# The sums of w_out made by accumulating DMAs in DRAM in place of VectorE's subtractions through SBUF

## Chip, cores and metric

The kernel runs on one core of one Trainium2 chip. The metric is the device time of one execution in microseconds (us). The kernel before takes 778.07 us (median of three runs, 777.9 to 778.26). A measurement of this kernel can tell a difference of about 0.2% from none.

## What is computed

One layer: a normalisation, a gated short convolution between two matrix products, a second normalisation and the residual. x is 1024 x 1024, w_in 1024 x 8192, w_out 2048 x 1024, all float32.

```python
u = rms_norm(h, pre_norm)
z, bg, cg, v = split(u @ w_in, 4)            # each 1024 x 2048
y = bg * causal_dwconv(cg * v, conv_w) * silu(z)
m = y @ w_out
out = h + rms_norm(m, post_norm)
```

## The kernel before

Both products are made by a scheme of seven products on halves (Strassen's, in Winograd's form): in place of eight half-size products, sums of the quarters of both operands are made, and seven products of those sums are combined. Two of the seven ("b" and "f") are cut once more by the same scheme into seven small ones (a' to g'). The matmuls work on float32 values that are split into a high and a low part: ScalarE writes the high part with a cast, VectorE subtracts it from the value to get the low part, and each product is three matmuls (low by high, high by low, high by high; L226 to L228, L798 to L800, L1138 to L1140, L1234 to L1236).

**First stage.** The 16 blocks c of 128 columns of y are made one after the other. For each there are two weight pairs, p = 2c (cg and v) and p = 2c + 1 (z and bg). The loop over `slots` is the order of the work: slots ("a", p), ("c", p), ("e", p), ("d", p), ("g", p), with the small products of b and f between them. Behind each product, `prepare` splits the weights of the slots to come (7 us ahead by a list of costs), `after` empties the PSUM bank, and further work is hung onto the slot by its name. All of this is written in program order; each engine runs its own instructions in that order (`tc.manual_schedule()`), and waits come from the buffers that instructions read and write.

- SyncE (SP) issues all but one of the DMAs: `fetch` the raw weights (L138), `y_done` the store of y (L291), and loads and stores of sums.
- GpSimd (POOL) makes the sums of the weights, `add_s` (L150 to L158) and `deep_sums` (L752 to L756), and a few multiplications (L260, L827, L1086).
- ACT's `snap` (L234) copies the PSUM bank of product a, c or e to SBUF before the next product is added to the same bank.
- The sums of w_out for the second stage are made on the side, one block j a pair, at p = 8 to 23 (`TODO`). At even p, VectorE makes four sums of the quarters b11, b12, b21, b22 of w_out (`fetch_t`, L330, four loads; `add_t`, L355 and L356, four subtractions and four stores to `t_d`). At odd p, GpSimd makes the sums for the small products of b and f (L326 and L342 to L351).
- SBUF work space is a ring of 36 pages of 128 x 512 float32.

**Second stage** (m = y @ w_out), from about 620 us. `units` of w_out sums (u) and y sums (y) are loaded (`load_unit`, L858), split (`split_pages`, ACT cast and VectorE subtraction at L162 and L163) into a pool of seven buffers "u", and multiplied (`out_mm`). Product "a" comes first (two halves h, four row tiles q), then `product_b` with the small products a', b', c', e', d', f', g' (`small_mm`, L1234 to L1236, and `small_add`, L1241). Around the start of it the program order is this:

1. end of the loop over slots: loads of A2, B3 and X; splits of B2, B1 and **A1**;
2. two more `fetch_unit`, then the loads of `gpost` (L1121), the post-norm weights spread over the partitions, one tile for each half of the columns;
3. products of ("a", 0); y sums on VectorE (L935, L936); `add_y` of the last block (L312 to L314); splits of **A2** and **A3**;
4. products of ("a", 1); split of **B3**; copies of the four banks of "a" to `acc`, that is C11 (L1196, ACT);
5. small products a', b', c', ...; behind each, `small_add` adds its bank to two rows of `acc`. a', c', d' and g' accumulate in one bank, which `small_add` reads after each.

```python
DEEP_C = {"a'": ("x'", 0, 0), "b'": ("y'", 0, 0), "c'": ("x'", 0, 1), ...
OUT_A = {"a'": ("A1", 0), ..., "b'": ("A2", 0), ..., "e'": ("A3", 0), "c'": ("A3", HH)}
OUT_B = {"a'": ("B1", 0), ..., "b'": ("B2", 0), ..., "c'": ("B3", 0), ...}
```

Of the kernel before, what the change touches and what calls it, by code (L numbers as in the profile page):

```python
# [12 lines left out]
ALU = mybir.AluOpType  # L13
# [4 lines left out]
DEEP_F = 3  # L18
# [5 lines left out]
def kernel(  # L24
# [16 lines left out]
    nc = tc.nc  # L41
    P = 128
    _, L, D = x.shape
# [4 lines left out]
    HB = 512  # L48
# [10 lines left out]
    wov = w_out[0].rearrange("(c p) n -> p c n", p=P)  # L59
# [13 lines left out]
    def page(name, dtype=F32, shape=(HB,)):  # L73

        return pages.tile([P, *shape], dtype, tag="pg", name=name, bufs=PAGES)
# [9 lines left out]
    CH = NC // 2  # L85
# [4 lines left out]
    t_d = dram.tile([P, 4, CH, HB], F32, tag="t_d", name="t_d")  # L90

    CQ = CH // 2
    tb_d = dram.tile([P, 2, 2, CQ, HB], F32, tag="tb_d", name="tb_d")
    tx_d = dram.tile([P, 2, CQ, HB // 2], F32, tag="tx_d", name="tx_d")
# [77 lines left out]
    def by_seven(z, c):  # L172

        return c >= DEEP if z == "b" else DEEP_F <= c < NC - 1
# [127 lines left out]
    def add_y(c):  # L302

        if c < CH:
            cv = done.pop(c)
            t = page(f"s3_{c}")
            nc.vector.tensor_sub(t, cv[:, :HB], cv[:, HB:])
            nc.sync.dma_start(s_d[:, SK["d"], c], t)
        else:
            cv, (t0, t1) = done.pop(c), far_y.pop(c)  # L310
            t2 = page(f"s4_{c}")
            nc.vector.tensor_add(t1, t1, cv[:, HB:])  # L312
            nc.vector.tensor_sub(t0, t1, t0)
            nc.vector.tensor_sub(t2, cv[:, :HB], t0)  # L314
            for k, t in zip("cef", (t0, t1, t2)):
                nc.sync.dma_start(s_d[:, SK[k], c - CH], t)

    ts = {}

    def fetch_t(j):  # L320

        if j >= CH:
            z, k = divmod(j - CH, CQ)
            ts[j] = [page(f"tb{n}_{j}") for n in (0, 1)]
            for n in (0, 1):
                nc.sync.dma_start(ts[j][n], wov[:, CH + k + n * CQ, z * HB : (z + 1) * HB])  # L326
            return
        ts[j] = [page(f"t{n}_{j}") for n in range(4)]
        for n, t in enumerate(ts[j]):
            nc.sync.dma_start(t, wov[:, j + n // 2 * CH, n % 2 * HB : (n % 2 + 1) * HB])  # L330

    def add_t(j, steps=range(4)):

        if j >= CH:
            z, k = divmod(j - CH, CQ)
            if 0 in steps:
                ts[j].append(page(f"t23_{j}"))
            b0, b1, t = ts[j]
            l, r = slice(0, HB // 2), slice(HB // 2, HB)
            for n in steps:  # L340
                if n == 0:
                    nc.gpsimd.tensor_sub(b0[:, r], b0[:, r], b0[:, l])  # L342
                    nc.sync.dma_start(tb_d[:, z, 0, k], b0)
                elif n == 1:
                    nc.gpsimd.tensor_sub(t[:, l], b1[:, r], b0[:, r])
                elif n == 2:
                    nc.gpsimd.tensor_sub(t[:, r], t[:, l], b0[:, l])
                    nc.sync.dma_start(tb_d[:, z, 1, k], t)
                else:
                    nc.gpsimd.tensor_sub(b1[:, l], b1[:, l], t[:, l])  # L350
                    nc.sync.dma_start(tx_d[:, z, k], b1[:, l])  # L351
            return
        t = ts[j]
        for n, a, b in [((1, 1, 0), (3, 3, 1), (0, 3, 0), (2, 2, 3))[n] for n in steps]:
            nc.vector.tensor_sub(t[n], t[a], t[b])  # L355
            nc.sync.dma_start(t_d[:, n, j], t[n])  # L356


    idle = small.tile([P, P], F32, tag="idle", name="idle", bufs=1)
# [501 lines left out]
    def fetch_unit():  # L861
        n = len(fetched)
        if n < len(UNITS):
            fetched.append(load_unit(*UNITS[n]))
# [87 lines left out]

    END = len(PAIRS) - 1

    TODO = {2 * DEEP_F + 2 + 2 * j + n: j + n * CH for j in range(CH) for n in (0, 1)}


    slots = [("a", 2), ("b", 2)]
    for p in range(2, len(PAIRS)):
        q = p + 1  # L960
# [35 lines left out]
    at, t = [], 0.0  # L996
# [6 lines left out]
    def prepare(n):  # L1003
        while ready[0] < len(slots) and at[ready[0]] < at[n + 1] + LEAD:
            slot = slots[ready[0]]
            if slot[2:]:
                z, i, c = slot
                deep_prep(z, c, i)
            elif slot[::-1] not in wt:
                split_w(*slot[::-1])  # L1010
            ready[0] += 1

    first_chunk("")
    for n, slot in enumerate(slots):
        if slot[2:]:
            z, i, c = slot
            deep_product(z, c, i)

            early = (z, i) in (("f", "c'"), ("f", "e'"))
            if early:  # L1020
                deep_after_f(c, i)
            if (z, i) != ("f", "c'"):
                prepare(n)
            if z == "f":
                if not early:
                    deep_after_f(c, i)
                continue
            deep_after(c, i)
            if (i, c) == ("f'", NC - 1):
                third_unit(0)  # L1030
            elif i == "g'" and c == NC - 1:
                nc.scalar.activation(sn[2 * c + 1, "a"], sn[2 * c + 1, "a"], AF.Silu)
            continue
        i, p = slot
        f7 = by_seven("f", p // 2)
        product(p, i)

        ahead = DEEP <= (p - (i == "a")) // 2 < DEEP_F and (i, p % 2) in (("d", 1), ("a", 0))
        for step in (after, prepare) if ahead else (prepare, after):
            step(*((n,) if step is prepare else (p, i)))  # L1040
        q, prev = p + 1, p // 2 - 1
        if p == 2:
            first_chunk(i)
        if i == "c":
            if p % 2 and p // 2 < DEEP:
                nc.scalar.activation(sn[p, "a"], sn[p, "a"], AF.Silu)
            if p % 2 == 0 and p in TODO:
                fetch_t(TODO[q])
            if p % 2 == 0 and p > 2:
                fetch_s(prev)  # L1050
            if p % 2 == 0 and p in TODO:
                add_t(TODO[p], [0, 1])
            if p % 2 == 0 and p // 2 >= DEEP:
                deep_sums("b", p // 2, 1)
        elif i == "e":
            add_s(q, "ecdf" if f7 else "ec")
            if f7 and p % 2 == 0:
                for part in (0, 1):
                    deep_sums("f", p // 2, part)
            if p % 2 and q in TODO:  # L1060
                fetch_t(TODO[q])
            if p in TODO and p % 2:
                add_t(TODO[p])
            elif p in TODO:
                add_t(TODO[p], [2, 3])
        elif i == "d":
            if p + 2 <= END:
                fetch(p + 2)
            if not f7:
                add_s(q, "d")  # L1070
            if p % 2 == 0 and p > 2:
                if f7:
                    split_w(q, "c")
                add_y(prev)
        elif i == "f":
            add_s(q, "f")
            if p == 2:
                add_y(0)
        elif i == "g":
            if p % 2 and q <= END and q // 2 >= DEEP:  # L1080
                deep_sums("b", q // 2, 0)
        elif i == "a":
            if p % 2 == 0 and prev >= DEEP:
                for t in (sn[p - 1, "c"], sn[p - 1, "a"]):
                    nc.scalar.activation(t, t, AF.Silu)
                nc.gpsimd.tensor_mul(cvs[prev][:, HB:], sn[p - 1, "c"], sn[p - 1, "e"])  # L1086
        if DEEP < NC and (i, p) in UNDER:
            UNDER[i, p]()
        if p == END - 1 and i in "cd":
            fetch_unit()  # L1090
        if p == END:
            if i in "acg":
                split_unit()
            elif i == "d":
                third_unit(2)
            if i in "ac":
                fetch_unit()
            elif i == "d":
                load_small("b", "B2")
            elif i == "f":  # L1100
                load_small("b", "A1")
                load_small("b", "B1")
                fetch_s(NC - 1)
            elif i == "g":
                for n in ("A2", "B3", "X"):
                    load_small("b", n)
                split_small("b", "B2")
                split_small("b", "B1")
                sums_y("b", "d", nc.vector)
                split_small("b", "A1")  # L1110
# [8 lines left out]
    gpost = [page(f"gpost{e}") for e in range(NE)]  # L1119
    for e in range(NE):  # L1120
        nc.sync.dma_start(gpost[e], post_norm[:, e * HB : (e + 1) * HB].broadcast_to([P, HB]))  # L1121
    acc = p2.tile([P, 2, TH, HB], F32, tag="acc", name="acc")
    jk = p2.tile([P, HB], BF16, tag="jk", name="jk")
    so = small.tile([P, NT, NE], F32, tag="so", name="so", bufs=1)
# [228 lines left out]
```

## Time and profile before

| what | value |
|---|---|
| median of three runs | 778.07 us (777.9 to 778.26) |
| the profiled execution, from its first to its last instruction (span) | 776.2 us; no other time of it is given |
| mean granted clock of TensorE | 0.997 of full speed |
| busy share: TensorE, VectorE, ScalarE, GpSimd | 99%, 80%, 56%, 53% |
| DMA | 127.17 MB, mean 164 GB/s |
| HBM read, written | 91.78 MB, 34.60 MB |

Times in the profile are us from the span's start unless marked ns. PE is TensorE, PEld its weight loads, DVE VectorE, ACT ScalarE, POOL GpSimd, SP SyncE; a q behind a name is that engine's issuing of DMAs and semaphore work, which counts as not busy. A row of a timeline gives start, length (of a run of equal instructions together), engine, line, operation, output and input, shape, the number of instructions and, in brackets, the idle time before and what ended it. A row of waits gives the sum of us, the number of times and the longest. A row of the table of stretches gives, for each engine, its busy time and, in brackets, its instructions, then TensorE's granted clock, the share of the DMA engines' time and GB/s. Matmuls overlap in the records, so the step from one start to the next is the time that each takes, not its recorded length.

### The profile page before, as it was taken

The page shows a single profiled execution, that of the slowest core. Times are in us where ns is not written, and L with a number is a line of the kernel's source. Part 1 is how long each engine was busy: PE and PEld are TensorE (multiplying, and loading weights), DVE is VectorE, ACT ScalarE, POOL GpSimd, SP SyncE. Part 2 cuts the span into 40 slices and gives each one's busy share as a digit, 9 for nine tenths or more (in the row PEclk, how much of TensorE's full clock was granted, in tenths as well). Part 3 has the DMA queues.
Part 4 walks back from the last instruction along what each step waited for, and adds up shares of the span by engine and source line. Part 5 has one row for each costly group of instructions (what it writes and reads, how often), then busy time and mean ns, then how long its engine had stood idle before and what let it go on. Part 6 is the DMA issues. An engine that isn't in the chain of part 4 may idle for free.

```text
span 776.2 us, 12058 instructions
## 1 busy us (share of the span) xinstructions
PE 766.0 (99%) x4086; PEld 661.8 (85%) x4086; DVE 618.4 (80%) x934; ACT 436.3 (56%) x810; POOL 413.2 (53%) x369
## 2 busy tenths in 40 slices
PE   8999999999999999999999999999999999999996
PEld 6888888888888888888888888888888889889985
DVE  5899786778687878788888887676778899966975
ACT  6764354766556565546465556555544576753821
POOL 2506786937575757575767667373737100850041
PEclk9999999999999999999999999999999999999998
DMA  9210531335463637364847456232325989966345
GB/s 310 71 55 1 149 96 55 96 109 181 138 204 117 210 111 230 111 208 131 257 136 250 138 174 178 96 109 96 115 89 166 336 275 378 309 196 210 112 169 184
DMA packets 115965, 127.17 MB, mean 164 GB/s; under 512 B 7432, under 2 KB 74304, under 8 KB 115904
## 3 DMA queue, kind: packets, MB, share of 16 engines
q1 hardware_dynamic: 115888, 126.41, 50.5%
q8 instruction: 32, 0.52, 0.3%
q14 instruction: 29, 0.24, 0.1%
q10 hardware_dynamic: 16, 0.00, 0.0%
HBM read 91.78 MB, written 34.60 MB: 163 GB/s over the span
## 4 chain that ended last, share of the span: by engine, by line
PE 98%; DVE 1%; DMA 1%; ACT 0%; POOL 0%; issue 0%; POOLq 0%; DVEq 0%; ACTq 0%
PE px L226 15%; PE px L227 15%; PE px L228 15%; PE pv L226 4%; PE pv L227 4%; PE pv L228 4%; PE po_x L1139 4%; PE po_x L1140 4%; PE po_x L1138 4%; PE px2b L800 2%; PE px2b L798 2%; PE px2b L799 2%; PE px2f L800 1%; PE px2f L799 1%; PE px2f L798 1%; PE pp L456 1%
## 5 line engine op out<-in xcount | busy, mean ns | idle before, releaser
L260 POOL TENSOR_TENSOR sne<-sne,cv 128x512 f32<-128x512 f32 x15 | 20.5, 1369 | 122.3 <-DVE cv L683 106.4
L187 ACT COPY beside<-raw 128x512 f32<-128x512 f32 x84 | 49.6, 590 | 29.2 <-DVE dwb1l L188 21.7
L154 POOL TENSOR_TENSOR se<-raw,raw 128x512 f32<-128x512 f32 x31 | 46.8, 1510 | 19.2 <-PE px L228 6.8
L234 ACT COPY sna<-px 128x512 f32<-128x512 f32 x30 | 17.6, 588 | 68.8 <-PE px L228 68.1
L226 PE MATMUL px<-u_d,wdl 128*128 128x512 f32 x124 | 48.7, 393 | 0.0
L226 PE MATMUL px<-u_a,wal 128*128 128x512 f32 x124 | 48.6, 392 | 0.0
L227 PE MATMUL px<-u_a,wah 128*128 128x512 f32 x124 | 48.6, 392 | 0.0
L227 PE MATMUL px<-u_d,wdh 128*128 128x512 f32 x124 | 48.5, 391 | 0.0
L226 PE MATMUL px<-u_g,wgl 128*128 128x512 f32 x124 | 48.4, 391 | 0.0
L227 PE MATMUL px<-u_g,wgh 128*128 128x512 f32 x124 | 48.4, 391 | 0.0
L227 PE MATMUL pv<-u_e,weh 128*128 128x512 f32 x124 | 48.4, 390 | 0.0
L228 PE MATMUL px<-u_d,wdh 128*128 128x512 f32 x124 | 48.4, 390 | 0.0
L226 PE MATMUL pv<-u_e,wel 128*128 128x512 f32 x124 | 48.4, 390 | 0.0
L228 PE MATMUL px<-u_a,wah 128*128 128x512 f32 x124 | 48.3, 389 | 0.0
L227 PE MATMUL px<-u_c,wch 128*128 128x512 f32 x124 | 48.2, 389 | 0.0
L228 PE MATMUL px<-u_c,wch 128*128 128x512 f32 x124 | 48.2, 389 | 0.0
L228 PE MATMUL pv<-u_e,weh 128*128 128x512 f32 x124 | 48.2, 389 | 0.0
L226 PE MATMUL px<-u_c,wcl 128*128 128x512 f32 x124 | 48.2, 389 | 0.0
L228 PE MATMUL px<-u_g,wgh 128*128 128x512 f32 x124 | 48.2, 389 | 0.0
L156 POOL TENSOR_TENSOR sc<-se,raw 128x512 f32<-128x512 f32 x31 | 44.9, 1448 | 5.8 <-issue 3.4
L158 POOL TENSOR_TENSOR sf<-raw,sc 128x512 f32<-128x512 f32 x31 | 46.3, 1493 | 0.0
L355 DVE TENSOR_TENSOR t<-t,t 128x512 f32<-128x512 f32 x32 | 45.8, 1450 | 0.3
(539 smaller groups left out, 2743.7 us busy)
## 6 DMA issues: line engine op xcount, KB each, us to landing
raw<-in_sc_w_in SPq DMA_DIRECT2D x128, 256.0 KB, 4.0
y_d<-cv SPq DMA_DIRECT2D x16, 512.0 KB, 3.2
s_d<-s SPq DMA_DIRECT2D x32, 256.0 KB, 2.9
t<-in_sc_w_out SPq DMA_DIRECT2D x32, 256.0 KB, 2.9
t_d<-t SPq DMA_DIRECT2D x32, 256.0 KB, 3.9
tb<-in_sc_w_out SPq DMA_DIRECT2D x16, 256.0 KB, 4.3
s<-y_d SPq DMA_DIRECT2D x16, 256.0 KB, 4.1
xr<-in_x SPq DMA_DIRECT2D x16, 256.0 KB, 3.8
```

The costliest lines, as they stand in the source:

```text
L154: nc.gpsimd.tensor_add(t, block(p, 1, 0), block(p, 1, 1))
L156: nc.gpsimd.tensor_sub(t, sums[p, "e"], block(p, 0, 0))
L158: nc.gpsimd.tensor_sub(t, block(p, 0, 1), sums[p, "c"])
L187: nc.scalar.copy(b, src)
L226: nc.tensor.matmul(ps, lo, UH[i][:, k], start=first and k == 0, stop=False, skip_group_check=True)
L227: nc.tensor.matmul(ps, hi, UL[i][:, k], start=False, stop=False, skip_group_check=True)
L228: nc.tensor.matmul(ps, hi, UH[i][:, k], start=False, stop=last, skip_group_check=True)
L355: nc.vector.tensor_sub(t[n], t[a], t[b])
L798: nc.tensor.matmul(ps, lo, uh, start=first and k == 0, stop=False, skip_group_check=True)
L1138: nc.tensor.matmul(ps, lo, u[:, 0, k], start=first, stop=False, skip_group_check=True)
L1139: nc.tensor.matmul(ps, hi, u[:, 1, k], start=False, stop=False, skip_group_check=True)
L1140: nc.tensor.matmul(ps, hi, u[:, 0, k], start=False, stop=last, skip_group_check=True)
```

## The change

The four sums of w_out for products d, e, g and c are no longer loaded to SBUF and subtracted. Their signs are turned (the second column half of w_out's sums and of the matching y sums change sign), so that e = b11 + b12, d = b12 + b22, c = e + b22 and g = c + b21. For each half h of the blocks there are six steps, one a pair from p = 8 (h = 0) and from p = 14 (h = 1):

- step 0: SP copies b11 to e and b12 to d, inside DRAM (1 MB each); step 2: SP copies e to c; step 4: SP copies c to g;
- step 1: b12 is added to e, and b22 to d, by four accumulating DMAs of 512 KB issued from GpSimd; step 3: b22 to c, two of them; step 5: b21 to g, two of them. They wait in a list `pending`, and `next_sum` issues one behind each slot.

GpSimd's own sums at odd p stay where they were. In `add_y` the three y sums of the far blocks are made with the other sign: a subtraction and two instructions of the form (a * -1) - b. The second half of the output columns comes out with the sign turned; gpost[1] is multiplied by -1 on ScalarE, right behind its load, to turn it back.

```diff
-            nc.vector.tensor_add(t1, t1, cv[:, HB:])
-            nc.vector.tensor_sub(t0, t1, t0)
-            nc.vector.tensor_sub(t2, cv[:, :HB], t0)
+            nc.vector.tensor_sub(t1, cv[:, HB:], t1)
+            nc.vector.scalar_tensor_tensor(t0, t1, -1.0, t0, op0=ALU.mult, op1=ALU.subtract)
+            nc.vector.scalar_tensor_tensor(t2, cv[:, :HB], -1.0, t0, op0=ALU.mult, op1=ALU.subtract)
...
     def fetch_t(j):
...
-        ts[j] = [page(f"t{n}_{j}") for n in range(4)]
-        for n, t in enumerate(ts[j]):
-            nc.sync.dma_start(t, wov[:, j + n // 2 * CH, n % 2 * HB : (n % 2 + 1) * HB])
...
     def add_t(j, steps=range(4)):
...
-        t = ts[j]
-        for n, a, b in [((1, 1, 0), (3, 3, 1), (0, 3, 0), (2, 2, 3))[n] for n in steps]:
-            nc.vector.tensor_sub(t[n], t[a], t[b])
-            nc.sync.dma_start(t_d[:, n, j], t[n])
...
+    pending = []
+
+    def out_sums(step, h):
+
+        js = slice(h * CQ, (h + 1) * CQ)
+        far = slice(CH + h * CQ, CH + (h + 1) * CQ)
+        b11, b12 = (wov[:, js, e * HB : (e + 1) * HB] for e in (0, 1))
+        b21, b22 = (wov[:, far, e * HB : (e + 1) * HB] for e in (0, 1))
+        d, e, g, c = (t_d[:, n, js] for n in range(4))
+        for to, src in ({0: ((e, b11), (d, b12)), 2: ((c, e),), 4: ((g, c),)}).get(step, ()):
+            nc.sync.dma_start(to, src)
+        for to, src in ({1: ((e, b12), (d, b22)), 3: ((c, b22),), 5: ((g, b21),)}).get(step, ()):
+            pending.extend((to[:, k : k + 2], src[:, k : k + 2]) for k in (0, 2))
+
+    def next_sum():
+
+        if pending:
+            to, src = pending.pop(0)
+            nc.gpsimd.dma_start(to, src, accum_op=ALU.add)
...
-    TODO = {2 * DEEP_F + 2 + 2 * j + n: j + n * CH for j in range(CH) for n in (0, 1)}
+    TODO = {2 * DEEP_F + 3 + 2 * j: j + CH for j in range(CH)}
+    SUMS = {2 * DEEP_F + 2 + 6 * h + step: (step, h) for h in (0, 1) for step in range(6)}
...
         q, prev = p + 1, p // 2 - 1
+        if i == "c" and p in SUMS:
+            out_sums(*SUMS[p])
+        next_sum()
...
-            if p % 2 == 0 and p in TODO:
+            if q in TODO:
                 fetch_t(TODO[q])
...
-            if p % 2 == 0 and p in TODO:
-                add_t(TODO[p], [0, 1])
...
-            if p % 2 and q in TODO:
-                fetch_t(TODO[q])
-            if p in TODO and p % 2:
+            if p in TODO:
                 add_t(TODO[p])
-            elif p in TODO:
-                add_t(TODO[p], [2, 3])
...
     for e in range(NE):
         nc.sync.dma_start(gpost[e], post_norm[:, e * HB : (e + 1) * HB].broadcast_to([P, HB]))
+    nc.scalar.mul(gpost[1], gpost[1], -1.0)
```

More of the change, by code (lines that the diff above doesn't have):

```diff
@@ L320, in fetch_t @@
     def fetch_t(j):
[L322 to L327, printed above, removed]
-        ts[j] = [page(f"t{n}_{j}") for n in range(4)]
-        for n, t in enumerate(ts[j]):
-            nc.sync.dma_start(t, wov[:, j + n // 2 * CH, n % 2 * HB : (n % 2 + 1) * HB])
-    def add_t(j, steps=range(4)):
[L334 to L352, printed above, removed]
-        t = ts[j]
-        for n, a, b in [((1, 1, 0), (3, 3, 1), (0, 3, 0), (2, 2, 3))[n] for n in steps]:
-            nc.vector.tensor_sub(t[n], t[a], t[b])
-            nc.sync.dma_start(t_d[:, n, j], t[n])
@@ new lines, in fetch_t @@
+        z, k = divmod(j - CH, CQ)
+        ts[j] = [page(f"tb{n}_{j}") for n in (0, 1)]
+        for n in (0, 1):
+            nc.sync.dma_start(ts[j][n], wov[:, CH + k + n * CQ, z * HB : (z + 1) * HB])
+    def add_t(j, steps=range(4)):
+        z, k = divmod(j - CH, CQ)
+        if 0 in steps:
+            ts[j].append(page(f"t23_{j}"))
+        b0, b1, t = ts[j]
+        l, r = slice(0, HB // 2), slice(HB // 2, HB)
+        for n in steps:
+            if n == 0:
+                nc.gpsimd.tensor_sub(b0[:, r], b0[:, r], b0[:, l])
+                nc.sync.dma_start(tb_d[:, z, 0, k], b0)
+            elif n == 1:
+                nc.gpsimd.tensor_sub(t[:, l], b1[:, r], b0[:, r])
+            elif n == 2:
+                nc.gpsimd.tensor_sub(t[:, r], t[:, l], b0[:, l])
+                nc.sync.dma_start(tb_d[:, z, 1, k], t)
+            else:
+                nc.gpsimd.tensor_sub(b1[:, l], b1[:, l], t[:, l])
+                nc.sync.dma_start(tx_d[:, z, k], b1[:, l])
```

## The prediction

> **What bounds the kernel now.** I read the busy shares first, then TensorE's own waits, then a table of stretches, one for each pair of weight blocks, and last the order of events around each place that the edits touch.
>
> ```profile
> span 776.2 us, 12058 instructions
> ...
> PE 766.0 (99%) x4086; PEld 661.8 (85%) x4086; DVE 618.4 (80%) x934; ACT 436.3 (56%) x810; POOL 413.2 (53%) x369
> ```
> ```profile
> PE pk L414 <- DVE ve_pre L102: 1.8, 1, 1.8
> ```
>
> A busy TensorE need not be a fast one, so the 99% alone prove little. The list of its waits says more: it holds four rows, 3.7 us in all, of which this is the longest, all from the loading of x at the start. No row names a sum of w_out, a weight split or a load after that. The table of stretches then gives a test that the kernel makes by itself:
>
> ```profile
> core 0: us, PE busy (x) PEld busy (x) DVE busy (x) ACT busy (x) POOL busy (x), PEclk, DMA share, GB/s
> ...
> 197.30:234.60 37.30, 37.30 (x206) 32.47 (x205) 29.77 (x45) 20.97 (x39) 24.73 (x24) 1.00 0.52 165
> ...
> 533.10:570.40 37.30, 37.30 (x206) 32.47 (x205) 26.31 (x43) 20.98 (x39) 20.54 (x20) 1.00 0.34 107
> ```
>
> The first stretch has four of the subtractions that are to go (and four of GpSimd's), with their loads and stores; in the second all that work is over. VectorE has 3.5 us less to do there and the DMA share falls from 0.52 to 0.34, yet TensorE passes 206 matmuls in the same 37.3 us. So TensorE's own rate sets the time, and **a sum of w_out taken from VectorE is worth nothing by itself**. The change can only cost, where a new wait reaches TensorE.
>
> **Part by part.**
>
> *Removed.* The rows of the sums:
>
> ```profile
> L355 DVE TENSOR_TENSOR t<-t,t 128x512 f32<-128x512 f32 x32 | 45.8, 1450 | 0.3
> ```
> ```profile
> y_d<-cv SPq DMA_DIRECT2D x16, 512.0 KB, 3.2
> ...
> t<-in_sc_w_out SPq DMA_DIRECT2D x32, 256.0 KB, 2.9
> t_d<-t SPq DMA_DIRECT2D x32, 256.0 KB, 3.9
> ```
>
> That is 32 subtractions of 1.45 us, 45.8 us of VectorE, with 32 loads, 32 stores and 32 SBUF pages. By the table above their worth is 0: other work on VectorE was already hidden under TensorE.
>
> *Added in their place.* SyncE issues eight copies of 1 MB inside DRAM, GpSimd issues sixteen accumulating DMAs of 512 KB. The copies: step 0 sends two, ahead of a fetch of raw weights in the same queue. At the rate of the y_d store (512 KB in 3.2 us) 2 MB take 12.8 us; they are called one weight pair (37.3 / 2 = 18.7 us) before the DMAs that add to them, so these should find them landed. The copies of steps 2 and 4 in turn wait for additions issued a pair earlier; if one came late, SyncE's fetches of raw weights would queue behind it, and GpSimd's sums wait for those. The fetch behind them may land some us later than now; its reader on GpSimd has the pause shown next. I cost this at 0.
>
> The accumulating DMAs sit in GpSimd's queue, between sums that feed the splits. One of them is not in the trace: no DMA of this kernel is issued by GpSimd. Bounds for GpSimd's time: from below 0.33 us, what SyncE takes to issue one (row of gpost, below), from above 6.4 us, twice the 3.2 us in which the 512 KB of y_d land, if GpSimd were held until both operands are read. A gain below 0 is excluded, since no GpSimd instruction goes. I take about 2 us: nearer to the issue of a DMA than to its landing, but written out by a general engine.
>
> ```profile
> 173.90 1.41 POOL L1086 TENSOR_TENSOR cv<-snc,sne 128x512 f32<-128x512 f32 x1 [0.29 <-POOL sne L260]
> ...
> 178.18 1.74 POOL L154 TENSOR_TENSOR se<-raw,raw 128x512 f32<-128x512 f32 x1
> ...
> 186.25 0.75 POOL L753 TENSOR_TENSOR dsf<-dsf,sf 128x256 f32<-128x256 f32 x1
> ...
> 193.38 1.29 POOL L154 TENSOR_TENSOR se<-raw,raw 128x512 f32<-128x512 f32 x1 [1.40 <-PE px L228]
> ...
> 209.49 1.30 POOL L260 TENSOR_TENSOR sne<-sne,cv 128x512 f32<-128x512 f32 x1 [7.68 <-DVE cv L683]
> ```
> ```profile
> 187.59 0.62 ACT L162 CAST dwf1h<-dsf 128x512 fp32r<-128x512 f32 x1
> 189.11 0.59 ACT L234 COPY sna<-px 128x512 f32<-128x512 f32 x1 [0.90 <-PE px L228]
> ```
> ```profile
> 193.08 0.39 PE L226 MATMUL px<-u_c,wcl 128*128 128x512 f32 x1
> ```
>
> GpSimd alternates between a dense run (172 to 188 us) and a loose one with a pause of 7.7 us. At an odd pair the four DMAs of step 1 go out behind slots c, e, d and a: two in the loose run, two in the dense one, ahead of L1086. The ones in the loose run have 7.7 + 1.4 us. In the dense run the sums dsf come at 187.0; ScalarE casts them at 187.59, then snaps px (189.11, 0.59), and px must be read before product c adds to it at 193.08. Cast and snap take 0.6 each, so dsf may come some 4.9 us later before TensorE notices. The four L154 to L158 sums in the run also took 1.74 us beside VectorE's subtractions against 1.29 without: 4 x 0.45 = 1.8 us come back. So two DMAs may take 6.7 us, **3.3 us each**, before they cost anything. At 2 us the cost is 0; at 6.4 it is 12.8 - 6.7 = 6.1 us in each of the two pairs that have a step 1, 12.2 us in all.
>
> On this price the Trainium skill, SBUF — State Buffer, section "SBUF: two separate sides", speaks against the change: DMAs issued by GpSimd have descriptors that VectorE can lock out, 620 ns becoming about 3100 ns beside a copy. An estimate from its 3.1 us is 6.2 us for two, still inside 6.7; no run here shows it yet.
>
> *The sign put back on ScalarE.* This one edit of one instruction I think decides the case. gpost[1] is multiplied by -1 right behind the issue of its load, and in ScalarE's program order that is between the casts of A1 and of A2 in the output stage.
>
> ```profile
> L1121 SPq DMA_DIRECT2D gpost<-in_post_norm x2: 332/332/333, 637.3 to 637.9; - x2
> ...
> DMA to landing us min/median/max: 5.3/5.3/5.3
> ```
> ```profile
> 631.08 4.27 ACT L162 CAST oA_b<-ry_b 128x512 fp32r<-128x512 f32 x8 [2.85 <-issue]
> ...
> 642.50 2.18 ACT L162 CAST oB_b<-B_b 128x512 fp32r<-128x512 f32 x4 [4.24 <-DMA s_d<-s]
> 644.59 2.04 ACT L1196 COPY acc<-po_x 128x512 f32<-128x512 f32 x4
> ```
> ```profile
> 642.25 0.28 PE L1234 MATMUL pb_x<-oB_b,oA_b 128*128 128x256 f32 x1
> ...
> 648.01 0.28 PE L1234 MATMUL pb_x<-oB_b,oA_b 128*128 128x256 f32 x1
> ```
> ```profile
> 646.79 0.68 DVE L1241 TENSOR_TENSOR acc<-pb_x,acc 128x512 f32<-128x512 f32 x1
> ...
> 652.74 0.68 DVE L1241 TENSOR_TENSOR acc<-pb_x,acc 128x512 f32<-128x512 f32 x1
> ```
>
> The first four of the eight casts at 631.08 are A1's; they end at 631.08 + 4 x 0.534 = 633.2. The load of gpost[1] is issued at 637.9 and lands 5.3 us later, at 643.2. ScalarE now never asks for it; after the change it stands still from 633.2 to 643.2. Queued behind the multiplication, in order: four casts of A2, four of A3, four of B3, and the copies L1196 of the bank C11. VectorE's low parts of each wait for the casts. From 643.2: thirteen instructions at 0.53 make 650.1; the two copies that hold rows 0 and 1 at 0.51 make 651.1; VectorE's add L1241 onto those rows, 0.68, makes 651.8. The bank that it reads is the one into which the third small product (c', the matmul at 648.01) accumulates, so c' can't begin earlier; with a tenth for the handovers it begins at 651.9 where it began at 648.01. **TensorE loses 3.9 us.** Some of it falls in b' (A2's low parts come about as b' wants them, near 645.1, where b' begins), the rest ahead of c'.
>
> What is late next: from add a' to add c' VectorE took 5.95 us (646.79 to 652.74), so the add of c' would end near 657.7, and two products after 651.9 (2.88 us each: two of them lie between 642.25 and 648.01) TensorE asks for it at 657.7 as well. Even; nothing more is lost, and all that follows has the same distance to TensorE as before or more. Bounds: if c' were free of the add, it would still want the last low part of B3, at about 650.8 where the fourth block of c' stood at 649.1: 1.7 us. From above, add 1 us for a landing as late as the slowest loads of that stage.
>
> *Signs in y.* One tensor_tensor and two two-step instructions replace three tensor_tensors, eight times; VectorE's slack hides them, and without that cover it would be well under 1 us. At the last place they stand in the time in which ScalarE waits.
>
> **Sum.** 0 for what goes, 0 for copies and accumulating DMAs, 0 for the y sums, 3.9 for the wait: span 776.2 + 3.9 = 780.1. The median of the runs, 778.07, is 1.9 above the profiled span, so 782.0.
>
> **Rivals.**
>
> 1. *The wait is absorbed; not slower, 778.1.* The place is the same load. Counting back, c' starts on time if gpost[1] lands 3.9 us earlier, by 639.3, or 1.4 us after its issue. For it: ScalarE had 4.2 us of idle time ahead of B3. Against it: the loads quoted above take 2.9 to 5.3 us to land, and the issue can't move forward, since it stands in SyncE's order behind a store of y that VectorE's last chunk releases, long after the removed sums are over. 8%.
>
> 2. *GpSimd becomes late in pairs 8 to 19.* It decides from 3.3 us per accumulating DMA, and costs up to 12.2 us on top: 782.0 to 794.2; in the middle 788. For it: the dense run has no other pause. Against: the estimate of 2 us, and the freed VectorE. 14%.
>
> 3. *The clock falls in the gap.*
> ```profile
> 6.00:8.00 2.00, 0.30 (x3) 0.30 (x4) 0.97 (x3) 1.58 (x4) 0.76 (x2) 1.00 1.01 406
> ```
> Here TensorE idles for 1.7 us and the granted clock stays at 1.00; the gap ahead of c' would be about 3.2 us, longer than any in the trace. Were the clock halved for one small product after it, that product's 2.88 us would double: 784.9. 6%. Beside this stands the Trainium skill, TensorE: Matmul & The Clock Gate, section "What's actually happening": a free-running window of about 3.4 us without work puts the array back to half clock. By that rule a gap of 3.2 us falls just short, while one that a late landing stretches by 1 us can fill a window.
>
> 4. *Faster.* If TensorE's pitch were held back by the traffic that goes, the two stretches above would differ. They don't. 2%.
>
> **How the numbers follow.** The forecast, 782.0, has 70% and a range of its own from 779.8 (the loss of 1.7) to 783.1 (the landing 1 us later). With rivals 3 and half of 2 the range is 779.6 to 788.0; rival 1, the far half of 2 and a gain stay outside, 17% together. A measurement of this kernel tells apart about 0.2%, 1.6 us. So faster has 2%, within 0.2% has 8% (rival 1), slower has 90%.
>
> **What would show each step.** The wait: on ScalarE one instruction on gpost that waits for its load some 10 us, at about 643 us; behind it twelve casts without a pause; TensorE's waits with two new rows, small in pb_y and near 3 us in pb_x, which names VectorE's L1241 or ScalarE. The sums: chunks of 37.3 us with 206 matmuls between 197 and 533 us as before; L355 gone; GpSimd's pauses near 10 us of each 37 shortened but not closed. I am wrong if the chunks between 160 and 385 us become longer (rival 2), if ScalarE's wait stands there and TensorE shows no gap (rival 1), if the clock of the stage falls below 1.00 (rival 3), or if the load of gpost is issued at another time than 637 to 638 us.

## The result and the profile after

The changed kernel takes 796.51 us (median of four runs, 796.05 to 798.89) against 777.99: the ratio is 1.0241, 95% interval 1.0225 to 1.0257. It is slower by 18.5 us, where 4 were forecast and 10 were the upper end of the range. The profiled run is the longest of the four (798.89); its span is 797.1 us against 776.2, so it shows 20.9 us of loss where the median run has 18.5.

The busy shares after the change, from the page's first part, and all but the last two rows of TensorE's waits:

```profile
span 797.1 us, 11907 instructions
...
PE 777.0 (97%) x4086; PEld 668.3 (84%) x4086; DVE 606.0 (76%) x902; ACT 435.9 (55%) x811; POOL 421.9 (53%) x385
```
```profile
PE px L226 <- ACT sna L234: 5.4, 2, 3.1
PE pb_x L1242 <- DVE acc L1249: 3.4, 1, 3.4
PE px L226 <- DVE sne L253: 1.2, 3, 0.7
PE pw L403 <- DVE idle L369: 1.1, 1, 1.1
PE pk L423 <- DVE xa L512: 0.9, 1, 0.9
```

Three rows are new, the first three. The one of 3.4 us in pb_x is the forecast. The other two lie in the first stage, where a product c waits twice for a snapshot on ScalarE (5.4 us) and a product g three times for VectorE (1.2 us). But these three add up to 10 us and the span grew by 20.9. To find the rest I set the first matmul of each product of the two traces side by side; these are the places, after the loading of x at the start, at which the distance between them grows by more than 0.25 us from one product to the next:

```
first matmul of          before      after    later by
px, product g            209.70     210.12      0.42
px, product c            230.38     233.32      2.94
px2f, c' (behind c)      233.10     237.71      4.61
px, product g            339.55     344.95      5.40
px, product c            342.30     351.11      8.81
px2f, c' (behind c)      345.02     356.40     11.38
pv2f, e'                 345.73     357.53     11.80
px, product g            396.23     409.07     12.84
pb_x, c' (output stage)  648.01     665.38     17.37
pb_v, e'                 650.89     670.66     19.77
pb_x, d'                 653.77     673.83     20.06
```

So there are three main places (and a smaller one, 0.8 us, at the g of 409.07, which waits 0.66 us for VectorE), and at each of the three the product that starts late is also slow: the c at 233.32 takes 4.4 us instead of 2.72, the one at 351.11 takes 5.3, the c' at 665.38 takes 5.3 instead of 2.88. The granted clock says why. Stretches around the first two places (TensorE's busy time and count first, the clock behind POOL):

```profile
228.00:233.30 5.30, 3.10 (x15) 2.26 (x14) 4.25 (x5) 1.13 (x3) 5.14 (x6) 1.00 1.01 306
233.30:238.00 4.70, 4.68 (x14) 3.76 (x15) 3.53 (x6) 2.68 (x6) 2.47 (x3) 0.64 0.66 126
...
345.00:351.00 6.00, 2.98 (x12) 2.12 (x12) 4.23 (x5) 1.67 (x4) 5.84 (x7) 0.96 1.03 340
351.00:356.40 5.40, 5.29 (x13) 4.13 (x13) 3.61 (x6) 2.72 (x6) 2.56 (x3) 0.50 0.67 119
```

TensorE idles for 2.2 us of the first stretch and 3.0 us of the third, and in the stretch behind each gap the clock is 0.64 and 0.50. In finer steps the clock is at half for a length of its own, which need not begin with the gap or end with it: about 3.4 us from 234.4, when TensorE had been at work again for 1.1 us, and about 6.8 us from 350.4, when it still stood idle:

```profile
234.40:237.80 3.40, 3.40 (x10) 2.66 (x9) 2.43 (x4) 1.54 (x3) 1.37 (x2) 0.50 0.50 65
350.40:357.20 6.80, 6.09 (x16) 4.93 (x17) 4.00 (x6) 3.89 (x9) 3.16 (x4) 0.50 0.77 147
```

Of the 12.8 us that the first stage loses, about 4.2 are slow matmuls (2.94 to 4.61 and 8.81 to 11.38), of the 7.2 us in the output stage 2.4.

What makes the first gap is read backwards along the engines. ScalarE and GpSimd after the change:

```profile
232.17 0.62 ACT L162 CAST dwf1h<-dsf 128x512 fp32r<-128x512 f32 x1 [4.27 <-POOL dsf L762]
232.69 0.58 ACT L234 COPY sna<-px 128x512 f32<-128x512 f32 x1
```
```profile
190.07 1.32 POOL L365 DMA_DIRECT2D t_d<-in_sc_w_out  x1
198.08 1.16 POOL L365 DMA_DIRECT2D t_d<-in_sc_w_out  x1 [6.68 <-issue]
...
211.34 1.30 POOL L260 TENSOR_TENSOR sne<-sne,cv 128x512 f32<-128x512 f32 x1 [2.96 <-DVE cv L692]
212.57 1.17 POOL L365 DMA_DIRECT2D t_d<-in_sc_w_out  x1
219.22 1.16 POOL L365 DMA_DIRECT2D t_d<-in_sc_w_out  x1 [5.48 <-ACT beside L187]
```

Product c at 233.32 waits for the snap at 232.69, which stands in ScalarE's queue behind the cast of dsf, which waits 4.27 us for GpSimd. GpSimd is late because it has issued two accumulating DMAs in its dense run (212.57 and 219.22). Each issue takes only 1.2 us, but ahead of the **second of two GpSimd stands still**, here for 5.5 us and, in the loose run before, for 6.7. The line's own group, after:

```profile
L365 POOL DMA_DIRECT2D t_d<-in_sc_w_out x16 | 18.7, 1171 | 48.1 <-issue 42.6 <-ACT beside L187 5.5
```

The 48.1 us fall on eight of the sixteen. "issue" means that no engine that the profile shows was waited for; the one pause under "ACT beside" has the same place and length, so I take the name for a bystander's. What ends it had to be found by experiment.

The forecast wait is there too. gpost's load is issued at 650.2 and 650.8 and lands in 5.3; ScalarE, VectorE and TensorE in that place:

```profile
644.06 2.19 ACT L162 CAST oA_b<-ry_b 128x512 fp32r<-128x512 f32 x4 [2.85 <-issue]
656.23 0.63 ACT L1129 ACTIVATE gpost<-gpost 128x512 f32<-128x512 f32 x1 [9.98 <-DMA gpost<-in_post_norm]
656.77 2.17 ACT L162 CAST oA_b<-ry_b 128x512 fp32r<-128x512 f32 x4
...
663.00 2.02 ACT L1204 COPY acc<-po_x 128x512 f32<-128x512 f32 x4
```
```profile
664.64 0.68 DVE L1249 TENSOR_TENSOR acc<-pb_x,acc 128x512 f32<-128x512 f32 x1
```
```profile
665.38 0.58 PE L1242 MATMUL pb_x<-oB_b,oA_b 128*128 128x256 f32 x1 [3.37 <-DVE acc L1249]
```

A wait of 9.98 us (10 forecast), twelve casts, the copies, the add, and c' 0.06 us behind the end of the add. What releases the add is one step off the forecast, though. The two copies that it needs are done by 664.0; VectorE's twelve low parts, which stand ahead of it in VectorE's queue, run from 657.40 to 664.72:

```profile
657.40 2.50 DVE L163 TENSOR_TENSOR oA_b<-ry_b,oA_b 128x512 fp32r<-128x512 f32 x4 [4.77 <-ACT oA_b L162]
...
662.23 2.49 DVE L163 TENSOR_TENSOR oB_b<-B_b,oB_b 128x512 fp32r<-128x512 f32 x4
```

### The profile page after: what moved, and what is told of

It is laid out like the page before. It is cut to its first block, busy times and chain, and to the rows that moved or that the text cites. A ratio compares the mean times of both kernels' runs of the same rounds, so it can differ in the third digit from the quotient of the medians.

```text
span 797.1 us, 11907 instructions
## 1 busy us (share of the span) xinstructions
PE 777.0 (97%) x4086; PEld 668.3 (84%) x4086; DVE 606.0 (76%) x902; ACT 435.9 (55%) x811; POOL 421.9 (53%) x385
## 3 DMA queue, kind: packets, MB, share of 16 engines
q1 hardware_dynamic: 109360, 118.02, 45.8%
## 4 chain that ended last, share of the span: by engine, by line
PE 77%; POOL 6%; issue 5%; DVE 4%; DMA 4%; ACT 2%; POOLq 0%; SPq 0%; DVEq 0%; ACTq 0%
PE px L226 11%; PE px L227 11%; PE px L228 11%; PE pv L226 4%; PE pv L227 4%; PE pv L228 4%; PE po_x L1146 3%; PE po_x L1147 3%; PE po_x L1148 3%; DVE cv L692 1%; PE px2b L809 1%; PE px2b L808 1%; PE px2b L807 1%; PE pp L465 1%; PE po_v L1147 1%
## 5 line engine op out<-in xcount | busy, mean ns | idle before, releaser
L226 PE MATMUL px<-u_c,wcl 128*128 128x512 f32 x124 | 50.0, 403 | 5.4 <-ACT sna L234 5.4
L154 POOL TENSOR_TENSOR se<-raw,raw 128x512 f32<-128x512 f32 x31 | 48.8, 1575 | 8.6 <-PE px L228 5.4
L228 PE MATMUL px<-u_c,wch 128*128 128x512 f32 x124 | 49.9, 403 | 0.0
L227 PE MATMUL px<-u_c,wch 128*128 128x512 f32 x124 | 49.9, 402 | 0.0
L107 POOL TENSOR_TENSOR rs_post<-ve_post,minus_half 128x1 f32<-128x1 f32 x8 | 4.4, 551 | 80.5 <-DVE ve_post L104 75.2
L692 DVE SCALAR_TENSOR_TENSOR cv<-gpad,cw,cv 128x1024 f32<-128x1024 f32 x32 | 44.7, 1397 | 2.2 <-ACT cv L683 1.9
L156 POOL TENSOR_TENSOR sc<-se,raw 128x512 f32<-128x512 f32 x31 | 42.9, 1385 | 5.8 <-issue 3.4
```

Source lines behind the costliest of these rows:

```text
L154: nc.gpsimd.tensor_add(t, block(p, 1, 0), block(p, 1, 1))
L156: nc.gpsimd.tensor_sub(t, sums[p, "e"], block(p, 0, 0))
L226: nc.tensor.matmul(ps, lo, UH[i][:, k], start=first and k == 0, stop=False, skip_group_check=True)
L227: nc.tensor.matmul(ps, hi, UL[i][:, k], start=False, stop=False, skip_group_check=True)
L228: nc.tensor.matmul(ps, hi, UH[i][:, k], start=False, stop=last, skip_group_check=True)
L692: nc.vector.scalar_tensor_tensor(cvs[c], gpad[:, j : j + L], tap(c, j), cvs[c], op0=ALU.mult, op1=ALU.add)
```

## The experiments

The theory: two separate losses. GpSimd's DMAs pause for want of space for their descriptors, which delays the weight sums in pairs 9 and 15; ScalarE's wait for gpost delays c'. Each gap costs once more because the clock falls. The rivals: GpSimd's pauses are waits for the landing of the DMA before; SyncE's copies delay the raw weights; the output stage is late as a consequence of the first; products behind a gap are slow for another reason.

**The multiplication moved.**

```diff
-    nc.scalar.mul(gpost[1], gpost[1], -1.0)
...
-        ("e", 0): lambda: (splits("B2", "B1", "A1"), loads("B3", "X")),
+        ("e", 0): lambda: (splits("B2", "B1", "A1"), loads("B3", "X"), nc.scalar.mul(gpost[1], gpost[1], -1.0)),
```

> The multiplication of gpost[1] by -1 is moved from behind its load to the end of the work beside product e (half 0), some 50 us later. Theory (two separate losses; the one at 648 us comes from ScalarE's wait for the load and is 7.2 us in the profile of the changed kernel): the jump ahead of c' is gone, the two losses near 230 and 342 us stay, 796.5 - 7.2 = about 789.3. Rival (the output stage is late because loads and pages lag behind the first stage's losses): the jump at c' stays, about 796.

789.85 us (788.33 to 792.52), ratio to before 1.0154 (1.0130 to 1.0178). The step ahead of c' is gone, those near 230 and 342 us are not. Its profiled run, the longest of its four, has 13.6 us of loss in the first stage against 12.8 in the changed kernel. The output stage's loss is its own.

**More space for the descriptors.**

```diff
-PAGES = 36
+PAGES = 35
...
-    nc = bacc.Bacc("TRN2", target_bir_lowering=False, num_devices=1, dynamic_dma_scratch_size=1024)
+    nc = bacc.Bacc("TRN2", target_bir_lowering=False, num_devices=1, dynamic_dma_scratch_size=2048)
```

> The space for the descriptors of GpSimd's DMAs is doubled, 1024 to 2048 bytes a partition, paid for with one of the 36 pages (35). Theory (the second of two accumulating DMAs stands 5 to 7 us because its descriptors do not fit beside the first one's): these pauses of GpSimd go, an accumulating DMA costs its 1.2 us, the losses near 230 and 342 us go, 796.5 - 12.8 = about 784. Rival (a DMA of GpSimd waits for the landing of the one before, whatever the space): pauses and time stay, about 796.

784.80 us, ratio 1.0092 (1.0071 to 1.0112). GpSimd's group of the line:

```profile
L365 POOL DMA_DIRECT2D t_d<-in_sc_w_out x16 | 18.9, 1396 | 0.0
```

No idle time ahead of any of the sixteen, and no step in the first stage. The two of a pair go out one behind the other, so GpSimd does not wait for the first to land. Its control takes the page away and leaves the space alone:

```diff
-PAGES = 36
+PAGES = 35
```

> The control to the doubled descriptor space: the changed kernel with 35 pages and the space left at 1024 bytes. Theory (the space alone took the pauses away): pauses of 5 to 7 us ahead of the second of two accumulating DMAs as in the changed kernel, about 796. Rival (35 pages shift SyncE's loads or GpSimd's work so that the pauses vanish): about 784.

796.65 us. The pauses as before the mending (the idle time ahead of the line by what ended it, us and times):

```profile
L365 POOL DMA_DIRECT2D t_d<-in_sc_w_out x16: 1144/1164/1330, 189.9 to 399.9; - x16
...
  issue: 43.4, 7
  ACT sne L234: 6.7, 1
```

So the space, and not the pages, makes the difference of 12 us.

**Smaller DMAs.**

```diff
-            pending.extend((to[:, k : k + 2], src[:, k : k + 2]) for k in (0, 2))
+            pending.extend((to[:, k : k + 1], src[:, k : k + 1]) for k in range(4))
```

> Thirty-two accumulating DMAs of one block (256 KB) in place of sixteen of two blocks, one behind each slot as before, so they last twice as many slots. Theory (descriptor space): two or three of them fit, GpSimd pauses at most 1 to 2 us before one, most of the losses near 230 and 342 us go, 784 to 787. Rival (waits for the landing of the one before): twice as many waits of 4 to 6 us, the losses stay or grow, 796 or more.

783.65 us, ratio 1.0077 (1.0053 to 1.0101), a little under the expectation.

```profile
L365 POOL DMA_DIRECT2D t_d<-in_sc_w_out x32 | 29.1, 1033 | 0.0
```

Twice as many issues, 10 us more of GpSimd's time in all, and no pause; the first stage runs without a step. That speaks against the rival of the landing once more: thirty-two DMAs would have had more landings to wait for. The counter-test halves the space for these:

```diff
-    nc = bacc.Bacc("TRN2", target_bir_lowering=False, num_devices=1, dynamic_dma_scratch_size=1024)
+    nc = bacc.Bacc("TRN2", target_bir_lowering=False, num_devices=1, dynamic_dma_scratch_size=512)
```

> Accumulating DMAs of one block with half the descriptor space, 512 bytes a partition. Theory (space): the ratio of space to DMA is that of the changed kernel again, so the second of two neighbours pauses 3 to 6 us again and the first stage loses time again, most where two stand together; with half the size per DMA 785 to 797. Rival (the size of a DMA, not the space, made the pauses): no pauses, 783.7.

834.97 us, ratio 1.0729 (1.0685 to 1.0774), far above the expectation. The pauses are back, on twenty of the thirty-two:

```profile
L365 POOL DMA_DIRECT2D t_d<-in_sc_w_out x32: 790/832/998, 190.1 to 450.5; - x32
...
  issue: 67.7, 16
  ACT dwf0h L186: 7.2, 2
  ACT sne L234: 5.5, 1
  ACT beside L187: 3.8, 1
```
```profile
PE px L226 <- ACT sna L234: 36.8, 5, 14.2
```

The sum of the pauses is 84 us against 48. I had scaled the loss by the size of one pause; what counts is how many stand in one dense run. Ahead of the c that starts at 244.34 there are four, 16.4 us in all, and TensorE waits 13.9 us for it; the row above has five such gaps, all of product c behind the snap.

**No accumulating DMAs.**

```diff
-            nc.gpsimd.dma_start(to, src, accum_op=ALU.add)
```

> The accumulating DMAs are left out (the copies inside DRAM stay), so the sums of w_out hold only their first term. Theory: chunks of 37.3 us throughout the first stage, only the loss at c' stays, 778 + 7.2 = about 785, or 783 where the clock does not fall. Rival (the copies of 1 MB in SyncE's queue delay the raw weights and cause part of the loss near 230 and 342 us): part of the 5.0 and 7.4 us stays, 786 to 790.

783.69 us (783.58 to 783.85), ratio 1.0072 (1.0056 to 1.0087), and no step in the first stage. The copies in DRAM cost nothing, as costed: the raw weights that are fetched behind the first two come later, and GpSimd's first sum of them starts at 194.91 where it started at 193.38, but no product is late for it; and the mended versions above, with all their DMAs, are within about 1 us of this.

**The multiplication alone, in the kernel before.**

```diff
         nc.sync.dma_start(gpost[e], post_norm[:, e * HB : (e + 1) * HB].broadcast_to([P, HB]))
+    nc.scalar.mul(gpost[1], gpost[1], 1.0)
```

> The kernel before with one instruction more: gpost[1] is multiplied by 1.0 on ScalarE right behind its load. Theory (the wait for that load alone makes the loss in the output stage): the jump of 4.3 to 4.8 us ahead of c' and the slower c' behind it, 783.7 as in the run without accumulating DMAs. Rival (the jump needs the copies or the turned sums): 778.

784.09 us (783.61 to 785.59), ratio 1.0079 (1.0064 to 1.0094). One instruction of 0.63 us costs 5.9 us, and nothing else of the change is needed for it. c' starts 4.81 us late and e' 7.22 us late.

**The gap filled.**

```diff
+    nc.scalar.mul(gpost[1], gpost[1], 1.0)
...
-        if first:
+        if first and (of_, i) != ("b", "e'"):
             ob[which] = bank(f"p{of_}_{which[0]}")
...
+            if i == "c'":
+                ob["v'"] = bank("pb_v")
+                for _ in range(16):
+                    nc.tensor.matmul(ob["v'"][:, :P], idle, idle, start=True, stop=True, skip_group_check=True)
             small_mm("b", i)
```

> The kernel before with that multiplication by 1.0 and with 16 matmuls of zeros (about 0.19 us each, 3.0 us) put into the gap ahead of c', into a bank that e' starts anew. Theory (c' takes longer because the clock falls to half in the gap of 3.4 us): c' starts as late as without them, but takes 2.9 us again, the granted clock stays at 1.00, 783.7 - 1.4 = about 782.3. Rival (c' is slowed by waits for its operands, not by the clock): no change, 783.7.

782.52 us, ratio 1.0054 (1.0039 to 1.0069). c' starts 4.53 us late, as without the matmuls of zeros, but no later step follows. The stretch from 652.5 us, in the run with the multiplication alone and in this one:

```profile
652.50:657.00 4.50, 4.18 (x19) 4.18 (x20) 4.38 (x10) 2.28 (x4) 0.00 (x0) 0.50 0.84 281
```
```profile
652.50:657.00 4.50, 4.50 (x40) 4.50 (x39) 4.40 (x9) 2.28 (x4) 0.00 (x0) 1.00 0.81 268
```

The same 4.5 us pass 19 matmuls at a clock of 0.50 and 40 at 1.00. The matmuls of zeros change nothing that c' waits for, so the clock it was. The longest of the four runs, 782.68, is below the shortest of the four without them, 783.61.

The kept runs also show that the price of a gap is not fixed. In the table, "at half" is the time that the clock stays at 0.50 in or behind a gap, read in steps of 0.1 us; the last two columns give how long the product behind it takes there and in the kernel before (all in us):

| run | product | wait of TensorE | at half | product takes | before |
|---|---|---|---|---|---|
| changed kernel | c, 233.32 | 2.23 | 3.4 | 4.39 | 2.72 |
| changed kernel | c, 351.11 | 3.13 | 6.8 | 5.29 | 2.72 |
| 35 pages alone | c, 352.84 | 3.10 | 0 | 2.87 | 2.72 |
| changed kernel | c', 665.38 | 3.37 | 6.8 | 5.28 | 2.88 |
| multiplication alone | c', 652.82 | 3.36 | 6.8 | 5.29 | 2.88 |
| no accumulating DMAs | c', 652.34 | 3.37 | 3.4 | 4.26 | 2.88 |
| 256 KB DMAs, 512 bytes | c', 701.72 | 3.36 | 0 | 2.97 | 2.88 |

The slow stretch is 3.4 us, twice that, or absent, and the length of the gap does not decide which.

**Both losses mended.** First the smaller DMAs with the later multiplication, then the larger space with it (the diffs are those above together):

> The changed kernel with both mendings: accumulating DMAs of one block, and the multiplication of gpost[1] later. Theory (two separate losses and no gain): chunks of 37.3 us, no gap in the output stage, 778, the same as before, although VectorE has 46 us less to do. Rival (freed VectorE and SyncE are worth something once the waits are gone): below 776.5.

778.30 us (median of ten runs), ratio 1.0002 (0.9993 to 1.0012).

> The doubled descriptor space (2048 bytes, 35 pages) together with the later multiplication of gpost[1]. Theory: no loss in either place, 778, like the other mended version. Rival (two DMAs of 512 KB back to back still hold GpSimd for 2.4 us in its dense run and that reaches TensorE once the other loss is gone): 779 to 781.

778.14 us (ten runs), ratio 1.0004 (0.9994 to 1.0014). No version beats the kernel before. A chunk of the first of the two shows why:

```profile
197.30:234.60 37.30, 37.30 (x206) 32.47 (x205) 28.25 (x41) 20.98 (x38) 29.71 (x31) 1.00 0.75 186
```

206 matmuls in 37.3 us, as in both stretches of before, with the DMA share at 0.75 and GpSimd at 29.7 us.

## Why the prediction was wrong

- **What bounds the kernel: right.** Without its two losses the change is worth 0.0% (intervals of about 0.1% to either side), though VectorE is busy 25 us less over the span (618.4 to 593.8 in the first mended version). That is less than the 45.8 us of the removed subtractions: the new y sums take 1.9 us more (20.0 for 18.1), and some instructions that stayed became longer, such as the eight of L307, 10.3 us for 6.5.
- **The wait on ScalarE: right in place and nearly in size, with one link of the chain wrong.** 3.9 us forecast; in the changed kernel c' falls back by 4.4 us (17.37 late, where the output stage begins 12.97 late). The add came behind VectorE's twelve low parts (to 664.72) and not behind the copies (664.0). The changed y sums have no part in it: with the multiplication alone the step to c' is the same 4.35 us.
- **The step that failed: the price of an accumulating DMA, "I take about 2 us".** The issue takes 1.2 us, and a second one close behind the first stands still for 6.0 us more in the mean (48.1 us over eight): together 7.8 us for the two in the dense run (212.57 to 220.38), **3.9 us each**, above the 3.3 from which rival 2 was to decide. The working of that rival was sound. 7.8 us plus the 1.85 us by which the run began late (211.34 for 209.49) make 9.7; 6.7 were free; 3.0 are left, and product c starts 2.94 us later than before. The 1.85 us come through VectorE: the pause in the loose run put GpSimd's next issue and sums beside a subtraction of VectorE at 198.32, which took 2.54 us where it took 0.41 at 198.41 before; which of them slowed it is not tested. What I priced was one DMA by itself; what mattered was the room that two need together, and the size of that room (1024 bytes) stood in the kernel's last function, unread. The upper bound of 6.4 us each did contain the measured price, but I gave the case 14%. The lock-out by VectorE that the prediction quotes does not show: the longest of the sixteen issues took 1.33 us, and the pauses went away with the larger space while VectorE's work stayed.
- **The clock: a rival that came true, at 6%.** It was set against one gap, and in this execution the clock fell at all three. It makes 6.6 of the profiled run's 20.9 us. The estimate for one place, 2.9 us, is near the 2.4 in c'. I let a rule about the length of the gap hold the chance down. The rule of the Trainium skill, TensorE: Matmul & The Clock Gate, section "What's actually happening", asks for an idle window of about 3.4 us; here the clock was at 0.64 behind a gap of 2.2 us, so the trace does not agree with it as a lower limit. That gaps of 3.10 and 3.36 us left the clock at 1.00 in other runs, and that the slow stretches last 3.4 or 6.8 us, would fit a window that runs on by itself; no run here sets the window, so this is not shown.
- **The copies, the sums' signs, SyncE: right at 0.** The copies land 6.1 to 9.9 us after their issue, inside the pair (18.7 us) that they have.
- Together these make the measured time: in the profiled run 8.6 us of gaps and smaller steps and 4.2 us of slow clock in the first stage, 4.8 and 2.4 in the output stage, 20.0 of 20.9 us. The remaining 0.8 us comes behind the last computation, which starts at 792.30 for 772.24, again 20.06 us later.

Open is what decides how long the clock stays at half. It is the likely source of the spread between runs of one kernel: with the multiplication moved, the longest run (792.52) has the lowest mean clock, 0.992, and the shortest (788.33) the highest, 0.997. The profiles show one execution each, so where the other runs lost time is not shown.

## What to carry to other kernels

On an engine's queue, price an added instruction together with its neighbours: a resource that one DMA fits into, descriptor space here, may hold up the second, and the profile calls that idle time "issue" or names a bystander. Any wait put ahead of other work in an in-order queue costs what is queued behind it, so an instruction on freshly loaded data belongs where the data have long landed. And where TensorE is the bound, a gap of 2 to 3.4 us can cost more than its own length: here between 0.1 and 2.6 us more, by how long the clock stayed at half.

## What was not expected of the hardware

- Judged by the pauses, one accumulating DMA of 512 KB fits 1024 bytes a partition of descriptor space and two do not; two fit 2048. Two of 256 KB fit 1024 and not 512. In the changed kernel the second of two is issued 6.3 to 8.7 us after the first, where one lands in 5.9 to 8.3. The issue takes 1.2 us for 512 KB, 0.8 to 1.1 us (medians) for 256 KB, longer (1.4 and 1.0 in the mean) where it need not pause.
- Such a DMA lands in 6.2 us (512 KB), about twice the 3.2 us in which the store of y lands its 512 KB. The Trainium skill, DMA: Bandwidth & Descriptors, section "Anatomy of one DMA — SWDGE (gpsimd) path", gives a fit of 2.0 us plus the bytes at 436 GB/s for a DMA issued by GpSimd; an estimate from it is 3.2 us, half of what was measured here with the addition.
- The clock stays at half for 3.4 us, for twice that, or not at all, behind gaps of one length (table above). With 16 matmuls of zeros, 128 columns each, in a gap of 3.4 us it stayed at 1.00.
